# Moving the query norm's factor from the rotated queries into the softmax exponent

## The chip, the cores and the metric

One NeuronCore of a Trainium2 chip runs the whole program. The metric is the device time of one execution in microseconds, as the median of several runs; one further execution is recorded by the hardware profiler. Lower is better.

## The reference

A two-layer hybrid network over 512 latent tokens and 256 context tokens of width 1024. The first layer mixes with grouped-query attention (16 query heads, 4 key heads, head width 64), the second with a gated linear recurrence; each is followed by a SwiGLU network. The part that matters here:

```python
def rms_norm(x, w):
    xf = x.astype(jnp.float32)
    y = xf * lax.rsqrt(jnp.mean(xf * xf, axis=-1, keepdims=True) + NORM_EPS)
    return (y * w.astype(jnp.float32)).astype(x.dtype)
...
    def queries(h):
        q = (h @ w_q).reshape(b, t, ATTN_KV_HEADS, ATTN_GROUP, HEAD_DIM).transpose(0, 2, 3, 1, 4)
        return rms_norm(q, q_norm)
    q_l = apply_axial_rope(queries(h_lat), rope)
...
def gqa_attend(q, k, v):
    s = jnp.einsum('bkgqd,bksd->bkgqs', q, k) * (HEAD_DIM ** -0.5)
    p = jax.nn.softmax(s, axis=-1).astype(v.dtype)
    return jnp.einsum('bkgqs,bksd->bkgqd', p, v)
```

The factor `rsqrt(mean(q*q)+eps)` is one number for each token and head. Weight, rotation and the product with the keys are linear in the query, so the number can be applied to the scores of that token and head instead.

## The kernel before, in words

All products with weights are done in three passes (`mm3`, lines 112 to 114): high part times high part, high times low, low times high. A weight tile is loaded raw, cast to its high part on ScalarE (line 88) and its low part is the difference, mostly on VectorE (line 91). For the query weights there are three buffers of each part, and two tiles for each of four groups of heads.

**Query projection.** For each of 4 groups of heads and each of 3 pairs of token tiles (`tp`), 48 matmuls fill one PSUM bank with 128 tokens x 2 x 4 heads x 64. Four such banks rotate. `q_first` then normalises, rotates and splits the queries; its `second` transposes them on TensorE (line 592) and casts them into `qT` (line 595, ScalarE) three calls later. In group 0 the same work for the keys (`k_first`) stands between. `qk_norm_rope` squares the bank on ScalarE (line 510), sums per head on VectorE (513), and makes the factor from a scale-and-add (514), a square root on ScalarE (515), a reciprocal and one refinement step (516 to 520), all on 128x8. It writes the normalised queries `qhat` (522), one buffer only. The rotation is two VectorE products with the cosines (532), four GpSimd products with the sines (537) and a sum (541); context tokens (`tp == 2`) have one product with the weight (526). A cast (585) and a difference (586) give the two parts of the transposed operand.

**Attention.** 96 units, one for each head and tile of 128 tokens. A unit is: scores on TensorE into one of two PSUM buffers `s2` (645, 646), the negated row maximum on VectorE (689), the exponential with that maximum as bias and its sum on ScalarE (691), the reciprocal of the sum on VectorE (692), the scaling of the 128x768 probabilities on GpSimd (693). Three units later the probabilities are transposed on TensorE (703) and split into two parts on ScalarE (88) and VectorE (91); six units later they meet the values (714, 715). The products with the output weights of the group before and other small work fill in between. GpSimd also makes the low parts of the output weights and of the attention outputs (91).

The order on each engine is set when the program is built, by program order and readiness; each engine then runs its list in order.

Of the kernel before, what the change touches and what calls it, by code (L numbers as in the profile page):

```python
# [8 lines left out]
F32 = mybir.dt.float32  # L9
F32R = mybir.dt.float32r  # L10
U8 = mybir.dt.uint8
AF = mybir.ActivationFunctionType
ALU = mybir.AluOpType
AX = mybir.AxisListType
PSUM = bass.MemoryType.PSUM

P = 128
# [5 lines left out]
NT = T // P  # L23
NLT = NL // P
EPS = 1e-6
HEADS = 16
KVH = 4
HD = 64
# [19 lines left out]
def kernel(  # L48
# [10 lines left out]
    PE, DVE, ACT, POOL = nc.tensor, nc.vector, nc.scalar, nc.gpsimd  # L59
# [20 lines left out]
    def bank(name):  # L80
        return psums["pool"].tile([P, 512], F32, tag="b", bufs=psums["bufs"]["b"], name=name)
# [97 lines left out]
    def ada_mm(pa, mv, k):  # L179
        for j, m in enumerate(mv):  # L180
            PE.matmul(pa[32 * j : 32 * (j + 1)], cpad[:, k], m, start=(k == 0), stop=(k == KT - 1))

    def ada_put(pa, rows, dst, bias, nch, nk):
        n = nch * nk * 32
        w = min(n, P)
        ACT.copy(rows[0:w, 0 : max(n, P)], pa[0:w])
        pt = bank("pta")
        for i in range(0, n, P):
            PE.transpose(pt[:, i : i + w], rows[0:w, i : i + P], ident[0:w, 0:w])
        cols = pt[:, 0:n].rearrange("p (c k r) -> p c k r", c=nch, r=32)[:, :, :, 0:2]  # L190
        DVE.tensor_tensor(dst, cols, bias.unsqueeze(3).to_broadcast([P, nch, nk, 2]), op=ALU.add)
# [5 lines left out]
    def ada_chunk(ch, pa, rows, load):  # L197
        pa = (bank("pa") if pa is None else pa)[:, 0:256]
        for k in range(KT):
            raw = load(f"adw{ch}{k}")  # L200
            dma(raw, ada_w[0, k * P : (k + 1) * P, ch * D : (ch + 1) * D])
            r4 = raw.rearrange("p (b j n) -> p b j n", b=2, j=4)
            ada_mm(pa, [r4[:, :, j] for j in range(4)], k)
            yield
        ada_put(pa, rows(), modc[0][:, ch : ch + 1], ada_bias(0, ch, 1), 1, KT)
# [123 lines left out]
    qst = pool("qkvst", qes, side="right")  # L329
# [41 lines left out]
    for t in range(NT):  # L371
        r = rs0[:, t : t + 1]
# [44 lines left out]
    for k in range(KT):  # L417
        ps = s2(f"ptx{k}")
        for t in range(NT):
            PE.transpose(ps[:, t * P : (t + 1) * P], xt[t][:, k * P : (k + 1) * P], ident)  # L420
        h = stp.tile([P, T], F32, name=f"xhT{k}")
        if k % 2:
            ACT.copy(h, ps[:, 0:T])
        else:
# [3 lines left out]
    kraw = [qst.tile([P, 2, 256], F32, tag="kraw" if tp else "qsin", bufs=2 if tp else 1, name="kraw")  # L428
            for tp in range(NT // 2)]
# [38 lines left out]
    keep = pool("attkeep", att)  # L468
# [3 lines left out]

    qT = [qt_tile(g) for g in range(KVH)]
    kTt = keep.tile([P, 2 * KVH, T], F32R, name="kT")
    kTh = [kTt[:, g] for g in range(KVH)]
    kTl = [kTt[:, KVH + g] for g in range(KVH)]

# [4 lines left out]
    tabs = {}  # L482
    for nm, wsrc, sc in (("k", attn_k_norm, 1.0), ("q", attn_q_norm, HD ** -0.5)):
        w = qst.tile([P, HD], F32, name=f"w{nm}")
# [3 lines left out]
        cw = qst.tile([P, NLT, HD], F32, name=f"cw{nm}")  # L488
        sw = qst.tile([P, NLT, HD], F32, name=f"sw{nm}")
# [10 lines left out]
        tabs[nm] = (w, cw, sw)  # L500

    def qk_norm_rope(src, tp, nm, eng=POOL):
        w, cw, sw = tabs[nm]

        def tmp(tag, bufs=1):
            tt = qst.tile([P, 512], F32, tag=tag, bufs=bufs, name=tag)
            return tt.rearrange("p (t h d) -> p t h d", t=2, d=HD)

        sq = tmp("qrot", 2)
        ACT.activation(sq, src, AF.Square)  # L510
        sst = qst.tile([P, 3, 8], F32, tag="ss", bufs=2, name="ss")
        ss, sr, sa = sst[:, 0], sst[:, 1], sst[:, 2]
        DVE.tensor_reduce(ss, sq.rearrange("p t h d -> p (t h) d"), op=ALU.add, axis=AX.X)
        DVE.tensor_scalar(ss, ss, 1.0 / HD, EPS, op0=ALU.mult, op1=ALU.add)
        ACT.activation(sr, ss, AF.Sqrt)
        DVE.reciprocal(sr, sr)
        DVE.tensor_tensor(sa, sr, sr, op=ALU.mult)
        DVE.tensor_tensor(sa, sa, ss, op=ALU.mult)
        DVE.tensor_scalar(sa, sa, -0.5, 1.5, op0=ALU.mult, op1=ALU.add)
        DVE.tensor_tensor(ss, sr, sa, op=ALU.mult)  # L520
        qh = tmp("qhat")
        DVE.tensor_tensor(qh, src, ss.rearrange("p (t h) -> p t h", t=2).unsqueeze(3).to_broadcast([P, 2, 4, HD]),
                          op=ALU.mult)
        r = tmp("qrot", 2)
        if tp == 2:
            eng.tensor_tensor(r.rearrange("p t h d -> p (t h) d"), qh.rearrange("p t h d -> p (t h) d"),
                               w.unsqueeze(1).to_broadcast([P, 8, HD]), op=ALU.mult)
            return r
        sn = tmp("qsin")
        for tt in range(2):  # L530
            t = tp * 2 + tt
            DVE.tensor_tensor(r[:, tt], qh[:, tt], cw[:, t].unsqueeze(1).to_broadcast([P, 4, HD]), op=ALU.mult)
            sn5 = sn[:, tt].rearrange("p h (a b i) -> p h a b i", a=2, b=2)
            q5 = qh[:, tt].rearrange("p h (a b i) -> p h a b i", a=2, b=2)
            t5 = sw[:, t].rearrange("p (a b i) -> p a b i", a=2, b=2)
            for b in range(2):
                POOL.tensor_tensor(
                    sn5[:, :, :, b], q5[:, :, :, 1 - b],
                    t5[:, :, b].unsqueeze(1).to_broadcast([P, 4, 2, 16]), op=ALU.mult,
                )  # L540
        DVE.tensor_tensor(r, r, sn, op=ALU.add)
        return r
# [8 lines left out]
    def k_first(tp):  # L551
# [26 lines left out]

        return second

    def q_first(g, tp, ps):
        eng = DVE if g == KVH - 1 and tp == 2 else POOL
        r = qk_norm_rope(ps.rearrange("p (t h d) -> p t h d", t=2, d=HD), tp, "q", eng)
        qd = qst.tile([P, 2, 4, 2, HD], F32R, tag="sp", bufs=3, name="qd")
        DVE.tensor_copy(qd[:, :, :, g % 2], r)
        eng.tensor_tensor(qd[:, :, :, 1 - g % 2], r, qd[:, :, :, g % 2].bitcast(F32), op=ALU.subtract)

        def second():
            for tt in range(2):
                pt = bank("ptq")  # L590
                for j in range(4):
                    PE.transpose(pt[:, j * P : (j + 1) * P],
                                 qd[:, tt, j].rearrange("p a d -> p (a d)").bitcast(F32), ident)
                t = tp * 2 + tt
                ACT.copy(qT[g][:, :, t * P : (t + 1) * P], pt.rearrange("p (h t) -> p h t", h=4))

        return second
# [3 lines left out]
    apsum = psums["pool"].tile([P, 512], F32, tag="a", name="pa")  # L601
# [2 lines left out]
        return psums["pool"].tile([P, 512], F32, tag="q", bufs=psums["bufs"]["q"], name=name)  # L604

    dfill = Fill()
    dfill.add(ada_chunk(3, apsum, lambda: qst.tile([P, 256], F32, tag="arows", name="arows"), ring_raw))
    later = []

    def first(fn, *args):  # L610
        if len(later) == Q_LAG:
            later.pop(0)()
        later.append(fn(*args))

    pend = []
    for g in range(KVH):
        ws = []
        for i in range(2):
            src = attn_w_qkv[0, 512 * i : 512 * (i + 1), g * 256 : (g + 1) * 256].rearrange("(k p) n -> p k n", p=P)
            ws.append(load_split(src, [P, 4, 256], f"wq{g}{i}"))  # L620
        for tp in range(3):
            psf = qbank(f"q{g}{tp}")
            for tt in range(2):
                ts_ = slice((tp * 2 + tt) * P, (tp * 2 + tt + 1) * P)
                ks = list(range(KT)) if tt == 0 else list(range(4, KT)) + list(range(4))
                for k in ks:
                    wh, wl = ws[k // 4]
                    mm3(psf[:, tt * 256 : tt * 256 + 256], hn_hi[k][:, ts_], hn_lo[k][:, ts_],
                        wh[:, k % 4], wl[:, k % 4], k == ks[0], k == ks[-1])
            if g == 0:  # L630
                first(k_first, tp)
            first(q_first, g, tp, psf[:, 0:512])
            dfill.step(2)
    def key_tiles(t):
        return range(4, 6) if t >= NLT else range(NT)

# [46 lines left out]
    def scores(h, t):  # L683
        ps = early.pop((h, t), None)
        if ps is None:
            ps = score_mm(h, t)
        nk = len(key_tiles(t)) * P
        st3 = ap_.tile([P, 4], F32, tag="st3", bufs=4, name="st3")
        DVE.tensor_reduce(st3[:, 0:1], ps[:, :nk], op=ALU.max, axis=AX.X, negate=True)  # L689
        pf = ap_.tile([P, T], F32, tag="pf", bufs=4, name="pf")[:, :nk]  # L690
        ACT.activation(pf, ps[:, :nk], AF.Exp, bias=st3[:, 0:1], accum_out=st3[:, 1:2])  # L691
        DVE.reciprocal(st3[:, 2:3], st3[:, 1:2])  # L692
        POOL.tensor_scalar(pf, pf, st3[:, 2:3], 1.0, op0=ALU.mult, op1=ALU.mult)  # L693
        return pf
# [947 lines left out]
    sa, sb = scan_head(GH - 2), scan_head(GH - 1)  # L1642
# [73 lines left out]
```

## Time and profile before

| | before |
|---|---|
| median of 3 runs | 1841.82 us (1838.89 to 1844.04) |
| profiled execution: time, span | 1841.11 us, 1839.3 us |
| mean granted TensorE clock | 0.989 of 2.4 GHz |
| TensorE / VectorE / ScalarE / GpSimd busy | 96% / 72% / 46% / 37% of the span |
| query projection | from 76 to about 175 us |
| attention | from about 179 to 422 us |

Busy time is the sum of an engine's own instructions; a busy TensorE is not one at its peak, since its matmuls overlap. The 1.8 us between the profiled time and the span lie outside the program's instructions.

### The profile page before, as it was taken

To read this page: it belongs to the slowest core of one execution; us is meant where nothing else is said; L and a number is where in the kernel's file an instruction comes from. 1 tells how busy PE (TensorE), PEld (TensorE's weight loads), DVE (VectorE), ACT (ScalarE), POOL (GpSimd) and SP (SyncE) were. 2 spreads that over 40 slices of the span, in tenths; PEclk is the share of its full clock that TensorE was granted. 3 is DMA by queue.
4 is the path that set the end of the run, shared out by engine and by line. 5 is a ranking of instruction groups with operands and counts; after the bars stand their busy time and mean duration, and the time that the engine had idled before them with its cause. 6 is when DMAs were issued, how large, how long until landed. Compare 5 with 4: busy or idle time off the path is not lost.

```text
span 1839.3 us, 30682 instructions
## 1 busy us (share of the span) xinstructions
PE 1758.3 (96%) x11725; PEld 1606.6 (87%) x11725; DVE 1327.1 (72%) x2315; ACT 844.0 (46%) x1752; POOL 680.5 (37%) x609
## 2 busy tenths in 40 slices
PE   8989999999999999999999999999998889999997
PEld 6779678988899989898998979899897789999996
DVE  3576688888888788877766465665747698786764
ACT  4333787777533424242445323233333455554544
POOL 1244255445513314131315353344537254443420
PEclk9989999999999999999999999999999999999999
DMA  9433510002034243535331111122211123333322
GB/s 328 163 114 86 161 65 24 12 13 75 24 110 125 64 126 92 160 116 155 103 104 57 58 58 55 61 81 83 78 47 46 44 61 111 108 105 105 98 60 82
DMA packets 213458, 166.43 MB, mean 90 GB/s; under 512 B 7952, under 2 KB 190400, under 8 KB 213312
## 3 DMA queue, kind: packets, MB, share of 16 engines
q1 hardware_dynamic: 213024, 163.43, 29.1%
q8 instruction: 92, 1.51, 0.3%
q10 hardware_dynamic: 288, 1.05, 0.1%
q14 instruction: 54, 0.44, 0.1%
HBM read 162.36 MB, written 2.10 MB: 89 GB/s over the span
## 4 chain that ended last, share of the span: by engine, by line
PE 77%; DVE 11%; POOL 4%; ACT 4%; issue 2%; DMA 1%; POOLq 0%; SPq 0%; ACTq 0%; DVEq 0%
PE ffo L113 5%; PE ffo L114 5%; PE ffo L112 5%; PE x L112 4%; PE x L113 4%; PE x L114 4%; PE pt L703 3%; PE y L114 2%; PE y L112 2%; PE y L113 2%; PE lv L1504 2%; PE hz L112 2%; PE hz L113 2%; PE hz L114 2%; PE sc L645 1%
## 5 line engine op out<-in xcount | busy, mean ns | idle before, releaser
L1511 POOL TENSOR_TENSOR KD<-KD,tot 128x384 f32<-128x384 f32 x96 | 100.5, 1070 | 67.0 <-ACT kc L1494 65.4
L693 POOL TENSOR_SCALAR pf<-pf,st 128x768 f32<-128x768 f32 (+1 forms) x96 | 73.4, 767 | 128.1 <-DVE st L692 91.7
L676 DVE SCALAR_TENSOR_TENSOR hT<-ffo,modc,hT 128x512 f32<-128x512 f32 (+1 forms) x122 | 78.7, 650 | 53.3 <-PE ffo L114 53.3
L114 PE MATMUL ffo<-gh,wlo_w 128*128 128x512 f32 (+1 forms) x304 | 103.8, 342 | 0.0
L113 PE MATMUL ffo<-gl,whi_w 128*128 128x512 f32 (+1 forms) x304 | 103.5, 341 | 0.0
L112 PE MATMUL ffo<-gh,whi_w 128*128 128x512 f32 (+1 forms) x304 | 102.5, 340 | 0.0
L1494 ACT COPY kc<-KD 128x256 f32<-128x256 f32 x112 | 42.9, 413 | 102.4 <-POOL KD L1511 37.1
L91 DVE TENSOR_TENSOR ptl<-pt,pth 128x384 fp32r<-128x384 f32 (+1 forms) x160 | 79.8, 524 | 12.5 <-ACT pth L88 11.2
L235 DVE SCALAR_TENSOR_TENSOR adacc<-adw,csil,adacc 128x512 f32<-128x512 f32 x98 | 84.6, 873 | 5.0 <-DMA adw<-in_ada_w_dram 4.7
L1511 DVE TENSOR_TENSOR QD<-QD,tot 128x256 f32<-128x256 f32 x96 | 57.1, 635 | 41.2 <-PE lv L1504 40.5
L88 ACT CAST pth<-pt 128x384 fp32r<-128x384 f32 (+1 forms) x160 | 69.9, 461 | 34.3 <-PE pt L703 22.5
L689 DVE TENSOR_REDUCE st<-sc 128x1 f32<-128x768 f32 (+1 forms) x96 | 74.2, 773 | 15.3 <-PE sc L646 12.5
L691 ACT ACTIVATE pf<-sc,st 128x768 f32<-128x768 f32 (+1 forms) x96 | 73.4, 765 | 19.2 <-DVE st L689 18.3
L703 PE MATMUL pt<-ident,pf 128*128 128x128 f32 x448 | 72.2, 275 | 5.1 <-DVE ptl L91 3.8
L112 PE MATMUL ffo<-gh,foh 128*128 128x512 f32 (+1 forms) x186 | 71.5, 384 | 0.0
L113 PE MATMUL ffo<-gl,foh 128*128 128x512 f32 (+1 forms) x186 | 71.0, 382 | 0.4 <-DVE gl L91 0.4
L114 PE MATMUL ffo<-gh,fol 128*128 128x512 f32 (+1 forms) x186 | 70.8, 381 | 0.0
L1504 PE MATMUL lv<-QD,kc 128*128 128x128 f32 x448 | 64.2, 288 | 5.7 <-DVE QD L1511 2.5
L1504 PEld LDWEIGHTS lv<-QD,kc 128*128 128x128 f32 x448 | 59.1, 194 | 10.1 <-issue 4.7
L113 PEld LDWEIGHTS ffo<-gl,whi_w 128*128 128x128 f32 x304 | 58.3, 192 | 7.1
L114 PEld LDWEIGHTS ffo<-gh,wlo_w 128*128 128x128 f32 x304 | 58.2, 191 | 6.6
L703 PEld LDWEIGHTS pt<-ident,pf 128*128 128x128 f32 x448 | 51.3, 140 | 14.4 <-issue 6.6
(1104 smaller groups left out, 6777.2 us busy)
## 6 DMA issues: line engine op xcount, KB each, us to landing
adw<-in_ada_w_dram SPq DMA_DIRECT2D x40, 512.0 KB, 4.5
adw<-in_ada_w_dram SPq DMA_DIRECT2D x80, 256.0 KB, 2.8
raw_hz<-in_hgrn_w_in_dram SPq DMA_DIRECT2D x14, 512.0 KB, 3.8
adr<-in_ada_w_dram SPq DMA_DIRECT2D x16, 256.0 KB, 4.5
adr<-in_ada_w_dram SPq DMA_DIRECT2D x8, 512.0 KB, 6.6
raw_wq<-in_attn_w_qkv_dram SPq DMA_DIRECT2D x8, 512.0 KB, 4.8
raw_wo<-in_attn_w_o_dram SPq DMA_DIRECT2D x8, 512.0 KB, 3.6
raw_hv<-in_hgrn_w_in_dram SPq DMA_DIRECT2D x8, 512.0 KB, 4.5
```

What stands on the lines that cost most here:

```text
L91: (eng or DVE).tensor_tensor(lo, src, hi.bitcast(F32), op=ALU.subtract)
L112: PE.matmul(ps, ahi, bhi, start=first, stop=False, **kw)
L113: PE.matmul(ps, ahi, blo, start=False, stop=False, **kw)
L114: PE.matmul(ps, alo, bhi, start=False, stop=last, **kw)
L235: pin(DVE.scalar_tensor_tensor(a, raw, cc, a, op0=ALU.mult, op1=ALU.add))
L676: DVE.scalar_tensor_tensor(hT[o][:, a:e], ps, mcol(layer, ch, o, v), hT[o][:, a:e], op0=ALU.mult, op1=ALU.add)
L689: DVE.tensor_reduce(st3[:, 0:1], ps[:, :nk], op=ALU.max, axis=AX.X, negate=True)
L691: ACT.activation(pf, ps[:, :nk], AF.Exp, bias=st3[:, 0:1], accum_out=st3[:, 1:2])
L693: POOL.tensor_scalar(pf, pf, st3[:, 2:3], 1.0, op0=ALU.mult, op1=ALU.mult)
L703: PE.transpose(pt[:, i * P : (i + 1) * P], pf[:, (i0 + i) * P : (i0 + i + 1) * P], ident)
L1504: PE.matmul(ps[:, cs], kc[:, cs], mv, start=True, stop=True)
L1511: eng.tensor_tensor(view, view, f, op=ALU.mult)
```

## The change

For the queries, the normalised copy is gone. ScalarE copies the raw bank to SBUF (`raw`, in the one buffer of `qhat`) and squares it; VectorE sums the squares of each head into a kept table `rq`. The rotation works on the raw values: VectorE multiplies straight from PSUM with the cosines, GpSimd multiplies the copy with the sines. The seven small steps that make the factor from the sum are done once per group of heads on 128x6x4 (`q_scales`), after the first tile of the next group. In attention each unit has one more VectorE product, of the 128x1 negated maximum with the 128x1 factor, and the exponential takes that as its bias and the factor as its scale, a second per-partition operand. The keys go as before. Two small tiles share other buffers.

```diff
+    rq = keep.tile([P, NT, HEADS], F32, name="rq")
...
+        return rope(qh, tp, nm, eng)
+
+    def rope(qh, tp, nm, eng, raw=None):
+        w, cw, sw = tabs[nm]
+        raw = qh if raw is None else raw
...
-            eng.tensor_tensor(r.rearrange("p t h d -> p (t h) d"), qh.rearrange("p t h d -> p (t h) d"),
+            eng.tensor_tensor(r.rearrange("p t h d -> p (t h) d"), raw.rearrange("p t h d -> p (t h) d"),
...
-            q5 = qh[:, tt].rearrange("p h (a b i) -> p h a b i", a=2, b=2)
+            q5 = raw[:, tt].rearrange("p h (a b i) -> p h a b i", a=2, b=2)
...
+    def q_scales(g):
+        ss = rq[:, :, 4 * g : 4 * g + 4]
+        sr = qst.tile([P, 2, NT, 4], F32, tag="sr", name="sr")
+        sr, sa = sr[:, 0], sr[:, 1]
+        DVE.tensor_scalar(ss, ss, 1.0 / HD, EPS, op0=ALU.mult, op1=ALU.add)
+        ACT.activation(sr, ss, AF.Sqrt)
+        DVE.reciprocal(sr, sr)
+        DVE.tensor_tensor(sa, sr, sr, op=ALU.mult)
+        DVE.tensor_tensor(sa, sa, ss, op=ALU.mult)
+        DVE.tensor_scalar(sa, sa, -0.5, 1.5, op0=ALU.mult, op1=ALU.add)
+        DVE.tensor_tensor(ss, sr, sa, op=ALU.mult)
...
-        r = qk_norm_rope(ps.rearrange("p (t h d) -> p t h d", t=2, d=HD), tp, "q", eng)
+        src = ps.rearrange("p (t h d) -> p t h d", t=2, d=HD)
+        raw = qst.tile([P, 512], F32, tag="qhat", name="qraw")
+        ACT.copy(raw, ps)
+        sq = qst.tile([P, 512], F32, tag="qrot", bufs=2, name="sqq")
+        ACT.activation(sq, ps, AF.Square)
+        mine = rq[:, 2 * tp : 2 * tp + 2, 4 * g : 4 * g + 4]
+        DVE.tensor_reduce(mine, sq.rearrange("p (t h d) -> p t h d", t=2, d=HD), op=ALU.add, axis=AX.X)
+        if tp == 2:
+            pend.append(g)
+        r = rope(src, tp, "q", eng, raw.rearrange("p (t h d) -> p t h d", t=2, d=HD))
...
-    dfill.add(ada_chunk(3, apsum, lambda: qst.tile([P, 256], F32, tag="arows", name="arows"), ring_raw))
+    dfill.add(ada_chunk(3, apsum, lambda: qst.tile([P, 512], F32, tag="kraw", bufs=2, name="arows"), ring_raw))
...
+            if pend and tp == 0:
+                q_scales(pend.pop(0))
             dfill.step(2)
+    q_scales(pend.pop(0))
...
-        ACT.activation(pf, ps[:, :nk], AF.Exp, bias=st3[:, 0:1], accum_out=st3[:, 1:2])
+        scale = rq[:, t, h : h + 1]
+        DVE.tensor_tensor(st3[:, 3:4], st3[:, 0:1], scale, op=ALU.mult)
+        ACT.activation(pf, ps[:, :nk], AF.Exp, bias=st3[:, 3:4], scale=scale, accum_out=st3[:, 1:2])
```

## Rows read from the trace of the kernel before

**Rows 1.** Windows: stretch, busy (instructions) by engine, clock, DMA share, GB/s.

```profile
128.00:135.00 7.00, 1.86 (x16) 1.66 (x14) 5.51 (x12) 3.81 (x6) 3.29 (x5) 0.79 0.00 0
135.00:141.00 6.00, 6.00 (x37) 6.00 (x38) 4.01 (x10) 0.21 (x1) 2.45 (x3) 0.68 0.58 178
175.00:187.00 12.00, 8.46 (x67) 6.64 (x65) 6.99 (x14) 6.64 (x11) 1.28 (x1) 0.86 1.02 262
```

**Rows 2.** Waits, 76 to 182 us: total us, times, longest.

```profile
ACT ss L515 <- DVE ss L514: 32.8, 13, 4.8
...
PE q L113 <- DVE wlo_wq L91: 5.1, 1, 5.1
...
PE sc L645 <- DVE qhat L522: 3.5, 1, 3.5
...
PE pta L189 <- ACT kT L571: 1.8, 1, 1.8
...
PE ptk L567 <- ACT qT L595: 1.5, 1, 1.5
```

**Rows 3.** Timeline around the longest wait: start, duration, engine, line, operation.

```profile
128.26 1.05 ACT L88 CAST whi_wq<-raw_wq 128x1024 fp32r<-128x1024 f32 x1
...
133.61 1.22 DVE L91 TENSOR_TENSOR wlo_wq<-raw_wq,whi_wq 128x1024 fp32r<-128x1024 f32 x1
```

**Rows 4.** Timeline at the passage from projection to attention.

```profile
179.01 0.50 PE L645 MATMUL sc<-kT,qT 128*128 128x512 f32 x1 [3.54 <-DVE qhat L522]
...
186.24 0.90 ACT L691 ACTIVATE pf<-sc,st 128x768 f32<-128x768 f32 x1
```

**Rows 5.** VectorE groups by form, 76 to 182 us: busy, mean ns | idle before.

```profile
L522 DVE TENSOR_TENSOR qhat<-q,ss 128x512 f32<-128x512 f32 x12 | 8.3, 692 | 1.0
...
L517 DVE TENSOR_TENSOR ss<-ss 128x8 f32<-128x8 f32 x15 | 3.8, 252 | 0.5
```

**Rows 6.** Windows of the attention stage, four of 60 us.

```profile
181.00:241.00 60.00, 57.84 (x438) 42.65 (x437) 37.05 (x84) 45.61 (x99) 21.41 (x24) 0.98 0.55 169
241.00:301.00 60.00, 57.27 (x395) 51.32 (x394) 51.98 (x118) 44.42 (x107) 26.83 (x29) 1.00 0.06 19
301.00:361.00 60.00, 59.08 (x418) 53.92 (x417) 52.99 (x122) 45.13 (x107) 26.78 (x28) 1.00 0.06 19
361.00:421.00 60.00, 59.08 (x417) 53.85 (x416) 52.55 (x121) 45.64 (x110) 28.10 (x29) 1.00 0.07 19
```

**Rows 7.** VectorE in attention, 181 to 422 us: a group, then a wait.

```profile
L692 DVE RECIPROCAL st<-st 128x1 f32<-128x1 f32 x96 | 15.0, 157 | 15.6 <-ACT pf L691 14.9
...
DVE st L692 <- ACT pf L691: 14.9, 20, 1.6
```

**Rows 8.** Timeline of VectorE and GpSimd around 91 us.

```profile
91.15 1.25 DVE L517 TENSOR_TENSOR ss<-ss 128x8 f32<-128x8 f32 x1
92.44 0.17 DVE L518 TENSOR_TENSOR ss<-ss 128x8 f32<-128x8 f32 x1
92.64 0.17 DVE L519 TENSOR_SCALAR ss<-ss 128x8 f32<-128x8 f32 x1
...
91.09 1.30 POOL L586 TENSOR_TENSOR qd<-qrot,qd 128x512 fp32r<-128x512 f32 x1 [1.27 <-DVE qd L585]
```

**Rows 9.** GpSimd groups in attention, 181 to 422 us.

```profile
L693 POOL TENSOR_SCALAR pf<-pf,st 128x768 f32<-128x768 f32 (+1 forms) x94 | 72.5, 773 | 128.1 <-DVE st L692 91.7 <-PE pt L703 32.9 <-PE rx L671 1.4
L91 POOL TENSOR_TENSOR wlo_wo<-raw_wo,whi_wo 128x1024 fp32r<-128x1024 f32 x8 | 19.1, 2389 | 9.1 <-ACT whi_wo L88 9.1
L91 POOL TENSOR_TENSOR qT<-ofp,qT 128x768 fp32r<-128x768 f32 x4 | 7.4, 1842 | 2.0 <-ACT qT L88 2.0
L91 POOL TENSOR_TENSOR o<-ofp,o 128x768 fp32r<-128x768 f32 x3 | 5.5, 1847 | 1.9 <-ACT o L88 1.9
```

**Rows 10.** ScalarE by form, 1500 to 1840 us: with and without a per-partition scale.

```profile
L835 ACT ACTIVATE fy<-hT,cols 128x512 f32<-128x512 f32 x6 | 4.3, 713 | 0.0
...
L267 ACT ACTIVATE sq<-hT 128x512 f32<-128x512 f32 x5 | 3.2, 637 | 0.0
```

More of the change, by code (lines that the diff above doesn't have):

```diff
@@ L502, in qk_norm_rope @@
     def qk_norm_rope(src, tp, nm, eng=POOL):
-        w, cw, sw = tabs[nm]
         def tmp(tag, bufs=1):
@@ L523, in qk_norm_rope, with tmp @@
                           op=ALU.mult)
+        return rope(qh, tp, nm, eng)
+    def rope(qh, tp, nm, eng, raw=None):
+        w, cw, sw = tabs[nm]
+        raw = qh if raw is None else raw
+        def tmp(tag, bufs=1):
+            tt = qst.tile([P, 512], F32, tag=tag, bufs=bufs, name=tag)
+            return tt.rearrange("p (t h d) -> p t h d", t=2, d=HD)
         r = tmp("qrot", 2)
         if tp == 2:
-            eng.tensor_tensor(r.rearrange("p t h d -> p (t h) d"), qh.rearrange("p t h d -> p (t h) d"),
+            eng.tensor_tensor(r.rearrange("p t h d -> p (t h) d"), raw.rearrange("p t h d -> p (t h) d"),
                                w.unsqueeze(1).to_broadcast([P, 8, HD]), op=ALU.mult)
```

## The prediction

> **What bounds the kernel now.** The table of engines says TensorE, busy for 96% of the span, but that average hides two different stages that the change touches, so I read them separately.
>
> For the projection (76 to 175 us) I read the waits first. TensorE waits little, and in four places only: 5.1 us for the low part of a weight tile, 3.5 us before the first scores, 1.8 and 1.5 us for transposition banks that ScalarE had not yet emptied [rows 2]. The timeline gives the cause of the first: ScalarE had the high part of the tile finished at 129.3, but VectorE made the low part only at 133.61 [rows 3], because it was working off older query tiles. The other side is that ScalarE lost 32.8 us in its square roots, waiting in order for VectorE's small steps [rows 2]. So VectorE runs behind in this stage, and TensorE pays for it in a few places. The windows add a second price: in the 6 us after the long wait TensorE ran at a granted clock of 0.68, between its 1.2 and its 2.4 GHz [rows 1].
>
> For attention (about 181 to 422 us) I read the windows. In the last three windows of 60 us TensorE is busy for 57.3 to 59.1 us, VectorE for 52.0 to 53.0, ScalarE for about 45 and GpSimd for 27 to 28 [rows 6]. TensorE sets the pace, and VectorE has only 8.0, 7.0 and 7.4 us of idle time in each window. 96 units in 240 us are 2.5 us a unit, or 24 to a window. The reader is to see that this stage has two nearly full engines.
>
> **The projection, part by part.** For each of 12 query tiles VectorE loses the 128x512 product `qhat`, 0.69 us [rows 5], and six small steps of 128x8 that take 0.17 to 0.25 us each when nothing else happens [rows 5, 8], some 1.8 us in all, or 22 us in the stage. `q_scales` gives back 4 x 6 small steps of about 0.2 us, 5 us, which lie beside matmuls. The two cosine products now read PSUM; their size is the same, and I take their cost as unchanged. ScalarE gains a 128x512 copy for each tile; its nearest row is a 128x512 pass of 0.64 us [rows 10], 12 x 0.64 = 7.7 us, and loses 8 of 12 square roots with their waits (32.8 us for queries and keys together [rows 2]). The copy has to wait until GpSimd is done with the one buffer `qhat`, but GpSimd starts earlier now, since the sines wait for a copy and no longer for the factor. I cost these moves at nothing: the cover is ScalarE's waiting time, and without it 7.7 us would be the price of the copies.
>
> What TensorE gets back:
> - The 5.1 us wait. The high part still comes only at 129.3 (its buffer is freed by the group before), and the low part takes 1.22 us more [rows 3]. TensorE came to a halt 5.1 us before the low part's end at 134.83, at 129.7. If VectorE is free, it resumes at about 130.6: 0.9 us are left, 4.2 are gained. Without the halt the low clock goes too: 6 us at 0.68 are 1.9 us of work not done [rows 1]. Together 6.1.
> - The waits of 1.8 and 1.5 us, where ScalarE's evictions stand behind a square root: I take 2.5 of 3.3.
> - The passage to attention. The scores stood still for 3.54 us until `qhat` had read the last bank, at 179.0 [rows 4]. Now ScalarE's copy and square are the last readers for a context tile, about 1.3 us after the last matmul, so this wait goes. The queries' last operand is also ready some 4 to 5 us earlier, and the first exponential, at 186.24 [rows 4], follows it. TensorE idles for 3.5 of the 12 us from 175 to 187, at a clock of 0.86 [rows 1]. I take 4.5.
>
> Sum: 6.1 + 2.5 + 4.5 = 13.1 us. Bounds: 7 if the rest of the list lets VectorE still come late half of the time, 17 if all waits and the low clock go (5.1 + 3.5 + 1.8 + 1.5 + 1.9, and 3 for the clock and the earlier start at the passage).
>
> **Attention, part by part.** The exponential gets a second per-partition operand. The nearest rows are a 128x512 pass with a per-partition scale, 0.713 us, and one without, 0.637 [rows 10]: 0.08 us, 96 times, 7 us of ScalarE, which has 15 us idle in each window [rows 6]. I cost it at nothing; without that cover it is 7 us.
>
> VectorE gets 96 products of 128x1. The lower bound is the row of its reciprocal on the same shape, 0.157 us [rows 7]; steps that follow each other start 0.20 us apart [rows 8]. So 24 x 0.20 = 4.8 us in a window that has 7.0 to 8.0 idle [rows 6]. That alone fits.
>
> The upper bound comes from one row. A 128x8 product with both inputs in SBUF, L517, usually takes 0.17 us; at 91.15 it took 1.25 and ended at 92.40, just when GpSimd's L586, begun at 91.09, ended at 92.39 [rows 8]. The mean over its 15 is 0.252 [rows 5]. The new product is of this kind: maximum and factor both lie in SBUF. VectorE's large steps in attention (maximum, split, residual) have an input in PSUM, and the reciprocal has one input and kept its 0.157 us in the mean over 96 [rows 7], so VectorE has not paid for GpSimd in this stage so far.
>
> The Trainium skill, page "SBUF — State Buffer", section "Who interferes with whom", says the same as a rule: a VectorE instruction with two SBUF inputs shares a read path with GpSimd instructions that read SBUF, and the second to start waits for the whole of the first. The row of L517 agrees (1.25 us). By that rule the product waits whenever GpSimd is at work; by the row of the reciprocal it would not, and the sum would be the 13 us gain alone.
>
> Price of the waiting: a product that starts at a random moment meets, on the average, the sum over GpSimd's instructions of busy time times half their length, over 240 us [rows 9]: 72.5 x 0.39 + 19.1 x 1.19 + 7.4 x 0.92 + 5.5 x 0.92 = 62.9, so 0.26 us. With 0.20 for the step itself 0.46 us a unit, 11.0 us in a window.
>
> What stands behind the product on VectorE: the exponential of its own unit, and all that VectorE has next, the splits that TensorE's products with the values need and the reciprocals that GpSimd waits for (91.7 us of its waits end so [rows 9]). A score buffer is held until the exponential has read it, and there are two.
>
> How much is hidden: in the first window VectorE has 23 us idle, and I cost the products there at nothing. In the other three they need 11.0 each, against 8.0, 7.0 and 7.4 of idle time [rows 6]: 3.0 + 4.0 + 3.6 = 10.6 us over, if every idle moment can be used. If none can, it is 33. Much of the idle time can't: 14.9 us of it are reciprocals that wait for an exponential [rows 7], which starts later now. I take the middle, 22.
>
> **Sum.** Against the profiled execution of 1841.1 us, 0.7 below the median of the runs: 1841.1 - 13.1 + 22 = 1850. With the ends of both terms: 1841.1 - 17 + 10.6 = 1835 to 1841.1 - 7 + 33 = 1867.
>
> **Rivals.**
> - *Faster: the product finds its place.* The product isn't held by GpSimd at this size, or falls into moments when GpSimd rests. For it: GpSimd is busy for only 45% of a window [rows 6], and with 0.20 us a unit everything fits. Against it: L517's row. It decides below some 0.29 us a unit (24 x 0.29 = 7.0, the least idle window). Then only the gain is left: 1841.1 - 13.1 = 1828. Chance 0.20.
> - *No difference: the idle time takes most of it.* The products wait as costed, but VectorE's idle moments absorb them: +10.6 against -13.1, 1839. For it: TensorE has lists of other work (output weights) to go on with. Against it: VectorE's waits for ScalarE, which grow with it. Chance 0.27.
> - *Much slower: VectorE becomes the bound.* No idle time is usable and TensorE, halted for GpSimd's 2.39 us pieces, falls to its lower clock at times: 1841.1 - 13.1 + 33 = 1861 and above. Chance 0.10.
>
> My forecast, slower by about 8 us, has 0.43.
>
> **The numbers.** 0.3% of 1841.8, 5.5 us, is about what a measurement of this kernel can tell from no change; that is 1836.3 to 1847.3. Faster takes the first rival and a little of the second, 0.22; slower takes the forecast and the last rival without their low edges, 0.51; the same gets 0.27. The predicted time is 1850. The likeliest case alone spans 1844 to 1858. For 8 in 10 I go down to the faster rival, 1828, and up to 1862, leaving out about 0.1 at either end.
>
> **What would show it.** Right: in the profile after, the wait for the low part at 129.7 is below 1.5 us, ScalarE's square roots number 4 for the queries, the scores begin within 1 us of the last projection, and attention starts about 10 us earlier. Then in attention the new 128x1 product has a mean of 0.35 us or more, with single ones over 1 us that end when a GpSimd instruction ends; VectorE is busy for over 57 of 60 us, and TensorE's idle time grows. Wrong: the product's mean stays near 0.17 us and attention keeps its 240 us, or the order of the lists moves so that the waits of the projection come back elsewhere.

## The result: 0.3% slower, two changes that nearly cancel

The changed kernel takes 1846.91 us in the median of its runs (1842.87 to 1852.34) against 1841.67 for the kernel before in the same rounds: a ratio of 1.0029, with a 95% interval of 1.0019 to 1.0038. The forecast was 1850.

Behind the small number stand two large ones. From the first exponential to the last, the kernel before went from 186.2 to 421.8 us, 235.6 us; the changed one goes from 172.7 to 427.9, 255.2 us. Attention begins 13.5 us earlier and lasts 19.6 us longer. In the table "way" is the mean, over the 96 units, of the time from the end of a maximum to the start of its exponential, worked out from the single instructions of each trace; it is one of the two main witnesses below; the other is what TensorE waits for.

| | before | after |
|---|---|---|
| first exponential, us | 186.2 | 172.7 |
| attention, us | 235.6 | 255.2 |
| way, us | 0.39 | 1.02 |

**Projection after.** The windows that answer to [rows 1]:

```profile
128.00:135.00 7.00, 7.00 (x62) 7.00 (x61) 4.90 (x11) 2.79 (x6) 3.13 (x6) 1.00 0.46 149
135.00:141.00 6.00, 6.00 (x54) 6.00 (x53) 1.91 (x5) 2.07 (x4) 3.04 (x5) 1.00 0.00 1
```

TensorE is busy without a break where it had stood still for 5.1 us, and its granted clock is 1.00 where it was 0.79 and 0.68. The waits from 76 to 175 us, TensorE's first and then some of ScalarE's, answer to [rows 2]:

```profile
PE ptk L576 <- ACT qT L625: 2.5, 1, 2.5
PE q L112 <- DVE cols L463: 0.6, 1, 0.6
PE sc L678 <- ACT sqq L608: 0.5, 1, 0.5
...
ACT sr L595 <- DVE rq L594: 7.9, 4, 3.1
...
ACT qraw L606 <- POOL qd L616: 4.5, 1, 4.5
...
ACT qraw L606 <- POOL qrot L535: 2.7, 1, 2.7
```

No wait for a low part is left, ScalarE waits for 4 square roots of the queries (`sr`), and in their place stand single waits of the raw copy for GpSimd. One of TensorE's small waits has grown, from 1.5 to 2.5 us. The passage in the timeline (start, duration, engine, line, operation, idle time before), for [rows 4]:

```profile
166.86 0.50 PE L678 MATMUL sc<-kT,qT 128*128 128x512 f32 x1 [0.48 <-ACT sqq L608]
...
172.72 0.99 ACT L726 ACTIVATE pf<-sc,st,rq 128x768 f32<-128x768 f32 x1
```

The first scores wait 0.48 us instead of 3.54 and come 12.2 us earlier.

**Attention after.** Four windows of 60 us that end, as those of [rows 6] do, within 1 us of the stage's end:

```profile
187.00:247.00 60.00, 52.64 (x390) 40.76 (x389) 48.30 (x121) 46.16 (x106) 26.80 (x27) 1.00 0.36 115
247.00:307.00 60.00, 57.16 (x380) 50.02 (x381) 52.56 (x129) 41.57 (x95) 24.09 (x25) 1.00 0.06 19
307.00:367.00 60.00, 57.55 (x383) 50.38 (x384) 52.63 (x135) 43.70 (x99) 25.95 (x27) 1.00 0.04 10
367.00:427.00 60.00, 57.31 (x382) 50.01 (x379) 51.89 (x134) 43.46 (x99) 23.55 (x25) 1.00 0.03 10
```

TensorE is busy for 0.1, 1.5 and 1.8 us less in the last three windows than in those of [rows 6], and for 5.2 less in the first, which begins 14 us after the first exponential where that of [rows 6] begins 5 us before it. VectorE, third of the busy columns, is at 52 to 53 us in the last three, where it was before: it has more to do for each unit, units pass more slowly, and the two cancel. By the prediction's account it would be at 57 and more. The same over the whole stage, before and after:

```profile
186.20:421.80 235.60, 228.59 (x1632) 197.99 (x1625) 194.26 (x441) 177.39 (x419) 103.93 (x109) 1.00 0.17 52
172.70:427.90 255.20, 237.83 (x1636) 200.09 (x1629) 214.47 (x537) 186.66 (x419) 105.40 (x110) 1.00 0.16 52
```

TensorE's idle time has grown from 7.0 to 17.4 us; the rest of the 19.6 us shows as busy time of the same matmuls. VectorE works 20.2 us longer in a stage that is 19.6 us longer. These sums alone would fit an engine whose idle moments can't be used at all; one of the experiments below separates that from the other reading. What TensorE waits for is told by two rows, one of its weight loads (PEld) and one of its matmuls, before and then after: the scores wait until an exponential (`pf`) has read the score buffer, and the transpositions wait until VectorE's split (`ptl`) has read their bank.

```profile
PEld sc L645 <- ACT pf L691: 3.1, 9, 0.9
PE pt L703 <- DVE ptl L91: 3.4, 7, 1.1
...
PEld sc L678 <- ACT pf L726: 9.1, 22, 1.5
PE pt L738 <- DVE ptl L91: 7.5, 16, 1.1
```

Below they are called the score wait and the split wait. Loads and matmuls overlap, so the two don't add up to the loss; they show where it arises. The new product, as one line's instructions (shortest, median, longest ns), with those that waited for it, and then ScalarE's exponentials by form (busy, mean ns of one, idle time before them):

```profile
L725 DVE TENSOR_TENSOR st<-st,rq x96: 136/158/1594, 170.6 to 426.7; 128x1 f32<-128x1 f32 x96
...
  ACT pf L726: 34.4, 49
  POOL pf L728: 18.7, 12
```

```profile
L726 ACT ACTIVATE pf<-sc,st,rq 128x768 f32<-128x768 f32 x64 | 63.7, 995 | 33.0 <-DVE st L725 32.0 <-DVE st L727 0.9
```

The same group before, over its attention:

```profile
L691 ACT ACTIVATE pf<-sc,st 128x768 f32<-128x768 f32 x64 | 58.0, 906 | 17.6 <-DVE st L689 16.8 <-DVE st L692 0.3
```

The exponential is 0.089 us longer (995 - 906 ns), and ScalarE's wait ahead of the large ones has gone from 17.6 to 33.0 us. Two stretches of the timeline show what it waits for. First, GpSimd holds the product:

```profile
219.61 2.40 POOL L91 TENSOR_TENSOR wlo_wo<-raw_wo,whi_wo 128x1024 fp32r<-128x1024 f32 x1 [0.67 <-ACT whi_wo L88]
...
221.26 0.76 DVE L725 TENSOR_TENSOR st<-st,rq 128x1 f32<-128x1 f32 x1
...
222.12 0.99 ACT L726 ACTIVATE pf<-sc,st,rq 128x768 f32<-128x768 f32 x1 [0.54 <-DVE st L725]
```

The product ends at 222.02, GpSimd's piece at 222.01. Second, the product stands in VectorE's list behind a split that has nothing to do with it, and is then held as well:

```profile
284.06 0.95 DVE L722 TENSOR_REDUCE st<-sc 128x1 f32<-128x768 f32 x1
...
284.12 1.84 POOL L91 TENSOR_TENSOR qT<-ofp,qT 128x768 fp32r<-128x768 f32 x1
...
284.93 0.55 DVE L91 TENSOR_TENSOR ptl<-pt,pth 128x384 fp32r<-128x384 f32 x1
...
285.39 0.58 DVE L725 TENSOR_TENSOR st<-st,rq 128x1 f32<-128x1 f32 x1
...
286.07 0.99 ACT L726 ACTIVATE pf<-sc,st,rq 128x768 f32<-128x768 f32 x1 [1.24 <-DVE st L725]
```

The maximum is done at 285.01 and its exponential starts at 286.07. The split accounts for 0.38 us of that (the product starts at 285.39), and GpSimd's piece, which ends at 285.96, for most of the product's 0.58. In 87 of the 96 units some other step of VectorE stands between maximum and product (37 times one split, 19 times a reciprocal and a split), and the product starts 0.41 us after the maximum's end in the mean.

### The profile page after: what moved, and what is told of

Same layout as the page of the kernel before. It is cut to its first block, busy times and chain, and to the rows that moved or that the text cites. A ratio compares the mean times of both kernels' runs of the same rounds, so it can differ in the third digit from the quotient of the medians.

```text
span 1846.6 us, 30777 instructions
## 1 busy us (share of the span) xinstructions
PE 1765.2 (96%) x11725; PEld 1606.8 (87%) x11725; DVE 1326.5 (72%) x2351; ACT 856.9 (46%) x1756; POOL 678.9 (37%) x609
## 4 chain that ended last, share of the span: by engine, by line
PE 75%; DVE 13%; ACT 4%; POOL 3%; issue 3%; DMA 1%; SPq 0%; POOLq 0%; ACTq 0%; DVEq 0%
PE ffo L113 5%; PE ffo L114 5%; PE ffo L112 5%; PE x L112 4%; PE x L114 4%; PE x L113 4%; PE y L114 2%; PE y L112 2%; PE y L113 2%; PE lv L1539 2%; PE hz L112 2%; PE hz L113 2%; PE hz L114 2%; PE pt L738 2%; DVE QD L1546 1%
## 5 line engine op out<-in xcount | busy, mean ns | idle before, releaser
L726 ACT ACTIVATE pf<-sc,st,rq 128x768 f32<-128x768 f32 (+1 forms) x96 | 81.9, 853 | 35.8 <-DVE st L725 34.4
```

What stands on the lines that cost most here:

```text
L726: ACT.activation(pf, ps[:, :nk], AF.Exp, bias=st3[:, 3:4], scale=scale, accum_out=st3[:, 1:2])
```

## The experiments

Two theories. *VectorE's capacity*, that of the prediction: the products, lengthened by waiting for GpSimd, use up VectorE's idle time, and what doesn't fit is the loss. *The longer way*: VectorE has the time, but the score buffer, of which there are two, is held longer for each unit, because a second step, its place in the list and its waits lie between maximum and exponential. Each run was timed in 5 rounds beside the kernel before on the same chip, whose median there was 1841.4 to 1842.9 us, so the ratios are what is compared. A ratio is taken over all runs and can differ a little from the quotient of the medians (0.9918 for "no factor"). All of them:

| kernel | median us | ratio to before (95%) | attention us | way us |
|---|---|---|---|---|
| before | 1841.7 | 1 | 235.6 | 0.39 |
| after | 1846.9 | 1.0029 (1.0019 to 1.0038) | 255.2 | 1.02 |
| no factor | 1826.3 | 0.9910 (0.9897 to 0.9923) | 234.2 | 0.36 |
| operand only | 1828.1 | 0.9921 (0.9908 to 0.9934) | 236.5 | 0.35 |
| step off the chain | 1833.6 | 0.9954 (0.9940 to 0.9969) | 240.1 | 0.39 |
| one-input step | 1840.8 | 0.9993 (0.9984 to 1.0002) | 248.6 | 0.96 |
| product on ScalarE | 1845.5 | 1.0013 (1.0003 to 1.0022) | 251.8 | 0.86 |
| before with product | 1860.8 | 1.0107 (1.0089 to 1.0124) | 255.1 | 1.07 |
| product tied, one input | 1846.4 | 1.0029 (1.0018 to 1.0039) | 254.4 | 1.01 |
| product tied | 1855.7 | 1.0078 (1.0063 to 1.0093) | 263.4 | 1.17 |
| fixed list, no step | 1839.5 | 0.9985 (0.9973 to 0.9997) | 246.2 | 0.35 |
| fixed list, one input | 1845.5 | 1.0020 (1.0009 to 1.0030) | 252.3 | 0.53 |
| fixed list, product | 1854.4 | 1.0063 (1.0049 to 1.0076) | 263.0 | 0.64 |
| scale fused with maximum | 1830.4 | 0.9937 (0.9924 to 0.9949) | 239.2 | 0.35 |

**The two halves apart.** The changed kernel without the factor, then with the operand alone:

```diff
-        DVE.tensor_tensor(st3[:, 3:4], st3[:, 0:1], scale, op=ALU.mult)
-        ACT.activation(pf, ps[:, :nk], AF.Exp, bias=st3[:, 3:4], scale=scale, accum_out=st3[:, 1:2])
+        ACT.activation(pf, ps[:, :nk], AF.Exp, bias=st3[:, 0:1], accum_out=st3[:, 1:2])
     # second kernel: ..., bias=st3[:, 0:1], scale=ones[:, 0:1], accum_out=...
```

> The changed kernel without the 128x1 product and without the second operand of the exponential; the queries' norm factor is left out of the scores, the projection and the four factor computations stay. All theories that put the loss into the product or the operand expect the gain of the projection alone: 1841.7 - 13.5 = about 1828 us, with attention again about 236 us from the first to the last exponential. If the loss comes from the changed projection itself (its lists pushed into attention), it stays above 1840.

> The changed kernel without the 128x1 product, but with a second per-partition operand (a column of ones) in the exponential; the norm factor is left out of the scores. GpSimd theory (the product waits for GpSimd): within 3 us of the run without both, about 1829. Rival, ScalarE's operand (0.09 us on each of 96 exponentials, on the path): most of the loss remains, 1840 or more.

Measured 1826.3 and 1828.1. The projection's part is thus worth 0.9% of the time (0.0090 x 1841.7 = 16.6 us), and the operand's price, 0.0011 x 1841.7 = 2.0 us, is not clear of the two intervals. ScalarE's cover holds: 96 longer exponentials cost next to nothing.

The other way round, the product put into the kernel before:

```diff
-        ACT.activation(pf, ps[:, :nk], AF.Exp, bias=st3[:, 0:1], accum_out=st3[:, 1:2])
+        DVE.tensor_tensor(st3[:, 3:4], st3[:, 0:1], ones[:, 0:1], op=ALU.mult)
+        ACT.activation(pf, ps[:, :nk], AF.Exp, bias=st3[:, 3:4], scale=ones[:, 0:1], accum_out=st3[:, 1:2])
```

> The kernel before, whose queries are normalised, with a product of 128x1 by a column of ones on VectorE and that column as the exponential's second operand, so that only attention's part of the change is made. If the two parts add up: 1841.4 + 19 to 21 = about 1861. If the product only costs when attention starts early: 1850 or less.

Measured 1860.8, attention 255.1 us: 19.5 us more than before, as in the changed kernel. The halves add up within the intervals, and neither needs the other to explain it.

**GpSimd's share.** The product is replaced by a step of the same size that reads one input of SBUF:

```diff
-        DVE.tensor_tensor(st3[:, 3:4], st3[:, 0:1], scale, op=ALU.mult)
+        DVE.tensor_reduce(st3[:, 3:4], st3[:, 0:1], op=ALU.max, axis=AX.X)
     # and scale=ones[:, 0:1] in the exponential
```

> In place of the 128x1 product with two inputs in SBUF a VectorE maximum of 128x1 with one input, same place in the list, and a column of ones as the exponential's second operand; the norm factor is left out of the scores. GpSimd theory: the step takes 0.16 us every time, the 12 us of waiting for GpSimd go, and with them 8 us or more of the time: 1832 to 1838. Rival, the step itself (a further link between maximum and exponential, whatever its inputs): no change, 1845 to 1848.

The step's line in this kernel:

```profile
L725 DVE TENSOR_REDUCE st<-st x96: 125/144/155, 168.3 to 417.9; 128x1 f32<-128x1 f32 x96
```

None of the 96 is late, against 24 products over 0.3 us and the longest of 1594 ns after. Yet the time falls only from a ratio of 1.0029 to 0.9993, 6.6 us; 13.3 us (0.9993 against 0.9921) are left for a step that takes 0.14 us and waits for nobody. That is nearly all of its 96 x 0.14 = 14 us, as if not one of VectorE's idle moments, over 7 us in each window, could take it. Either that is so, or the price is that of the way.

**Time or way.** The same kernel with one word changed, so that nobody waits for the step:

```diff
-        ACT.activation(pf, ps[:, :nk], AF.Exp, bias=st3[:, 3:4], scale=ones[:, 0:1], ...)
+        ACT.activation(pf, ps[:, :nk], AF.Exp, bias=st3[:, 0:1], scale=ones[:, 0:1], ...)
```

> As the kernel with the one-input step and the operand of ones (1840.8 us), so without the factor, but the exponential takes the maximum itself as its bias: the step is still issued 96 times on VectorE and nobody waits for its result. If what the step costs is VectorE's time, 96 x 0.14 = 14 us less than VectorE's idle moments take up, the time stays near 1841. If it is the longer way from a maximum to its exponential, the time falls to that of the kernel with the operand alone, 1828 to 1831, and the mean way is 0.35 to 0.4 us again instead of 0.96.

Measured 1833.6, between the two. VectorE's list still has another step between maximum and step in 87 of 96 units, as with the one-input step, though not always the same one: a split alone in 51 units instead of 37. The windows over the whole attention of three kernels, operand only, step off the chain, one-input step:

```profile
172.70:409.00 236.30, 228.90 (x1631) 198.19 (x1623) 195.62 (x441) 184.07 (x417) 104.28 (x109) 1.00 0.18 56
```

```profile
173.00:413.30 240.30, 230.28 (x1636) 198.67 (x1636) 202.73 (x536) 185.62 (x418) 104.66 (x110) 1.00 0.17 56
```

```profile
170.50:418.90 248.40, 235.13 (x1634) 199.49 (x1623) 202.26 (x537) 186.41 (x417) 105.03 (x110) 1.00 0.17 54
```

The second and the third do the same work: VectorE is busy for 202.7 and 202.3 us in 536 and 537 instructions. The third takes 8.1 us longer, and what was changed is that its exponential waits for the step (it also begins 2.9 us earlier, so it ends only 5.6 us later). This is the run that tells the theories apart: of the step's 13.3 us, 7.2 (0.9993 - 0.9954) come with the longer way, and 6.1 (0.9954 - 0.9921) are there without it, through VectorE's time or the shifted lists, which this run doesn't separate.

Two more readings bear this out. From the first line to the second VectorE's busy time grows by only 7.1 us, since neighbouring records overlap; so even with no idle moment of use its time could hardly account for 13.3. And TensorE's score wait is 3.2 us with the operand alone, 3.8 with the step off the chain and 8.7 with the step on it, so it is indeed the score buffer that comes free later. The split wait stays at 3.5 to 4.3 in all three and grows to 7.5 only in the changed kernel, whose products GpSimd holds: that part makes VectorE late for its splits. A third score buffer would test the longer way directly; no run has one.

**Off VectorE altogether.** The product as a ScalarE copy with a scale:

```diff
-        DVE.tensor_tensor(st3[:, 3:4], st3[:, 0:1], scale, op=ALU.mult)
+        ACT.activation(st3[:, 3:4], st3[:, 0:1], AF.Copy, scale=scale)
```

> The product is made by ScalarE (a copy with the factor as scale), everything else as in the changed kernel. GpSimd theory: VectorE is as loaded as before the change, ScalarE has 96 x 0.2 = 19 us more in a stage where it idles for a quarter; 1828 to 1835, faster than both kernels. Rival, the longer link between maximum and exponential: the step on ScalarE is as long as on VectorE and the loss stays, 1843 or more.

Measured 1845.5, not measurably better than the changed kernel (1.0003 to 1.0022 against 1.0019 to 1.0038). VectorE has its time back and GpSimd can't hold this step, but the copy takes 0.296 us in the median and the way is 0.86 us. It fits the longer way: the score wait is 9.6 us, as in the changed kernel, and the split wait 2.7, below that of the kernel before. But ScalarE also has 28 us (96 x 0.296) more to do.

**The product's place in the list.** If the split ahead of the product is half of the way, a product right behind its maximum should win that back. First attempt: the other steps of VectorE in attention are made to follow the product in the order, and the reciprocal moves to the next unit:

```diff
-        DVE.tensor_tensor(st3[:, 3:4], st3[:, 0:1], scale, op=ALU.mult)
+        prod.append(DVE.tensor_tensor(st3[:, 3:4], st3[:, 0:1], scale, op=ALU.mult))
...
-        DVE.reciprocal(st3[:, 2:3], st3[:, 1:2])
+        norm_prev()          # the reciprocal and GpSimd's product of the unit before
...
+            behind(DVE.tensor_tensor(ptl[:, i0 : i0 + n, qs], src, hi.bitcast(F32), op=ALU.subtract))
```

> The changed kernel, with VectorE's other attention steps tied behind the product, so that the product stands right behind its maximum in VectorE's list; the reciprocal and scaling of a unit are written one unit later. List theory (in the changed kernel 75 of 96 products stand behind another VectorE step, mostly a split, 0.41 us in the mean, and the exponential waits for that): 0.4 us less between maximum and exponential and 6 to 12 us off the time, 1835 to 1841. Rival, the step alone: unchanged, 1845 or more.

> The same lists with the one-input VectorE maximum of 128x1 in place of the product, and a column of ones as the exponential's second operand; the norm factor is left out of the scores. List theory together with GpSimd theory: both delays are gone, only 0.16 us of step are left; 1829 to 1834. Rival, the step alone: 1840.

Measured 1855.7 and 1846.4. The attempt failed in its aim: in 50 of 96 units another step still stood in between, and the way was 1.17 us. It says nothing on the place. The pair does say again what GpSimd costs: 9.0 us (1.0078 - 1.0029).

Second attempt: the order of VectorE's steps in attention is fixed outright, as they are written, with the step right behind its maximum:

```diff
-        DVE.tensor_reduce(st3[:, 0:1], ps[:, :nk], op=ALU.max, axis=AX.X, negate=True)
-        DVE.tensor_tensor(st3[:, 3:4], st3[:, 0:1], scale, op=ALU.mult)
+        pin(DVE.tensor_reduce(st3[:, 0:1], ps[:, :nk], op=ALU.max, axis=AX.X, negate=True))
+        pin(DVE.tensor_tensor(st3[:, 3:4], st3[:, 0:1], scale, op=ALU.mult))
     # splits, sums, residuals and the reciprocal (behind the next maximum) are pinned too;
     # the one-input step in place of the product, or no step, in the other two
```

> VectorE's attention steps are fixed in one order (maximum of a unit, reciprocal of the unit before, splits, the rest), without the 128x1 step, with a column of ones as the exponential's second operand; the norm factor is left out of the scores. This is the base for the next two. If the order is as good as the free one, 1828; if it is worse by itself, up to 1845.

> The same fixed order with the one-input VectorE maximum of 128x1 right behind each unit's maximum, nothing between; the norm factor is left out of the scores. List theory (the place in the list made the step dear): 0 to 5 us more than the run without the step, since only 0.2 us are added between maximum and exponential. Rival, any separate step costs its 12 us: 10 us or more.

> The same fixed order with the real product right behind each maximum. GpSimd theory: 4 to 9 us more than with the one-input step, with single products over 1 us that end with a GpSimd instruction; list theory: in sum faster than the changed kernel's 1846.9 if the fixed order is not worse by itself. Rival to GpSimd: the same as the one-input step.

The first of them shows that the fixed order is itself 11.8 us worse (0.9985 against 0.9921) than the list it replaces, so it is no remedy. Inside it the place is right: the step starts 0.03 us behind the maximum, and the way grows by 0.18 us only. The step then costs 6.4 us (1.0020 - 0.9985), where it cost 13.3 in the free list. That a bad place is about half of the step's price is argued from this, not shown, since the two lists differ in everything else. The real product costs another 7.9 us (1.0063 - 1.0020). In these lists the loss arises at another place: the split wait is 6.9 us without the step, 13.4 with it and 21.3 with the product, while the score wait is 4.8, 4.2 and 6.6. So with a way of only 0.53 to 0.64 us the step and the product still cost 14 us in sum, and what grows is TensorE's wait for VectorE's splits, as the theory of VectorE's capacity has it. The product's line:

```profile
L731 DVE TENSOR_TENSOR st<-st,rq x96: 159/160/1778, 170.3 to 432.9; 128x1 f32<-128x1 f32 x96
```

**No step at all.** The factor can be applied while the maximum is taken, by one instruction that multiplies the scores in place in PSUM and keeps the least of the products; the factor gets a minus sign in `q_scales`, so the least is the negative of the greatest:

```diff
-        DVE.tensor_reduce(st3[:, 0:1], ps[:, :nk], op=ALU.max, axis=AX.X, negate=True)
-        DVE.tensor_tensor(st3[:, 3:4], st3[:, 0:1], scale, op=ALU.mult)
-        ACT.activation(pf, ps[:, :nk], AF.Exp, bias=st3[:, 3:4], scale=scale, accum_out=st3[:, 1:2])
+        DVE.tensor_scalar(ps[:, :nk], ps[:, :nk], rq[:, t, h : h + 1], None, op0=ALU.mult, op1=ALU.min,
+                          accum_out=st3[:, 0:1])
+        ACT.activation(pf, ps[:, :nk], AF.Exp, bias=st3[:, 0:1], scale=-1.0, accum_out=st3[:, 1:2])
```

> No separate step: the maximum over the scores is replaced by one VectorE instruction that multiplies the scores in PSUM with minus the factor, writes them back and keeps their minimum; the exponential takes that minimum as bias and minus one as scale. If the loss comes from the separate step in any of its forms (place in the list, waiting for GpSimd, length) the gain of the projection stays whole: 1825 to 1832, below both kernels. If writing 768 scores back to PSUM makes the instruction longer than the maximum's 0.95 us by more than 0.15 us, 1835 or more.

Its line, by instruction:

```profile
L723 DVE TENSOR_SCALAR_CACHE_REDUCE sc<-sc,rq x96: 475/1015/1027, 169.1 to 409.7; 128x768 f32<-128x768 f32 x64, 128x256 f32<-128x256 f32 x32
L723 DVE DVE_READ_ACCUMULATOR sc<-sc,rq x96: 82/141/145, 170.1 to 410.1; 128x1 f32 x96
```

Measured 1830.4, a ratio of 0.9937 (0.9924 to 0.9949): it beats both kernels, with the factor applied. The read of the accumulator follows at once, so nothing gets in between; the way is 0.35 us, and the longest instruction is 12 ns above the median, so GpSimd doesn't hold it. The exponential has no second per-partition operand here, so the kernel without the factor is the one to compare: some 5 us of the gain are paid for the longer pass (0.9937 against 0.9910), in which VectorE's instruction with its read takes 0.2 us more than the maximum.

## Why the prediction came out right, and which step did not

Sums below are differences of ratios times 1841.7 us; by the intervals of the two ratios each has 2 to 4 us of uncertainty either way.

**The projection, 13.1 us predicted.** The first exponential is 13.5 us earlier, and without the factor the kernel is 16.6 us faster. Term by term: the wait for the low part was to shrink to 0.9 us and is gone, and the clock is 1.00, as predicted. The passage: the wait of 3.54 us is 0.48. Of the two waits for transposition banks, one has gone (1.8) and one has grown to 2.5, so of the 2.5 us predicted there at most 0.8 are seen (1.8 + 1.5 - 2.5). The moves costed at nothing, copies and square roots, can't have cost much, as the start shows, though the copies do wait for GpSimd's use of their one buffer (4.5 and 2.7 us).

The cosine products were taken as unchanged. They are shorter. Shortest, median and longest ns of the 16 of the queries, before and after, and then of the 4 of the keys after:

```profile
L532 DVE TENSOR_TENSOR qrot<-qhat,cwq x16: 419/682/725, 87.6 to 172.4; 128x256 f32<-128x256 f32 x16
...
L541 DVE TENSOR_TENSOR qrot<-q,cwq x16: 405/415/426, 85.7 to 161.2; 128x256 f32<-128x256 f32 x16
...
L541 DVE TENSOR_TENSOR qrot<-qhat,cwk x4: 415/555/691, 79.1 to 91.4; 128x256 f32<-128x256 f32 x4
```

The shape is the same. With both inputs in SBUF, 10 of the 16 took 680 to 725 ns, each of them while GpSimd multiplied the same `qhat` with the sines, and the other six 419 to 426; the keys' after fall into the same two kinds, two and two. With one input in PSUM all 16 take 405 to 426, also the three that ran beside a product with the sines. So GpSimd no longer delays them, which is worth 2.8 us of VectorE's time.

**Attention, 22 us predicted, 19.6 measured, by the wrong road.** The step of the prediction that failed is "how much is hidden": products of 0.46 us a unit against VectorE's idle time, of which the step's own 0.20 us were to fit and the waiting for GpSimd was to overflow. The own 0.20 us did not fit: a step of 0.14 us that nothing holds costs 13.3 us. The waiting for GpSimd is real but half as long: the mean product took 0.28 us, 0.12 above the median of 0.158, where 0.26 of waiting was predicted. Its group in the profile after:

```profile
L725 DVE TENSOR_TENSOR st<-st,rq 128x1 f32<-128x1 f32 x96 | 26.9, 280 | 0.6
```

The estimate took a random moment, and that was right: GpSimd was at work when 41 of the 96 products started (43%; it is busy for 41% of the stage), and the rest of its instruction was 0.246 us in the mean over all 96, against 0.26 estimated. Two other things were not. A held product ends with GpSimd's instruction (all 24 products over 0.3 us do), so its own 0.158 us lie inside the waiting and do not come on top, as the row of L517 in the prediction already had it: 0.05 us in the mean. And eight products that started 0.07 to 0.08 us after a scaling of GpSimd's were not held at all, 0.07 in the mean. One of them:

```profile
195.66 0.92 POOL L728 TENSOR_SCALAR pf<-pf,st 128x768 f32<-128x768 f32 x1 [2.39 <-DVE st L727]
...
195.73 0.15 DVE L725 TENSOR_TENSOR st<-st,rq 128x1 f32<-128x1 f32 x1
```

The witness that the prediction named, a mean of 0.35 us or more, is missed, and so is the other, VectorE busy for over 57 of 60 us. Singles over 1 us that end with a GpSimd instruction are there, and TensorE's idle time has grown.

What the runs put in its place, for 21.9 us from no factor (0.9910) to the changed kernel (1.0029): 2.0 for the operand, 6.1 for a step that nobody waits for, 7.2 for the exponential's waiting for it, 6.6 for GpSimd's holding it. 13.3 of the 21.9 us are there with a step of 0.14 us that no engine disturbs. The prediction did list the exponential as standing behind the product, but gave that no price, and it took the product to follow its maximum at once, while in 87 of 96 units another step came first. That the 6.1 us are VectorE's time is likely, since the fused kernel pays 5 us for as much added busy time (194.3 to 201.5 us) and no added wait, but not shown.

The Trainium skill, page "SBUF — State Buffer", section "Who interferes with whom", has VectorE with two SBUF inputs share a read path with GpSimd, and VectorE with one input go free. These runs agree: the product at up to 1594 ns, the one-input step of the same size at 155 at most. The rule that the prediction took from there, that the second to start waits for the whole of the first, holds for the 24 late products and not for the eight above; there the measurement decides.

**The rivals.** "Faster, the product finds its place" needed less than 0.29 us a unit; the product took 0.28 and the kernel was slower all the same, so its condition was the wrong one. "The idle time takes most of it" was 8 us too low. "VectorE becomes the bound" missed its 1861, and TensorE's granted clock stayed at 1.00. Its condition, that no idle moment is of use, is not refuted by VectorE's 52 us in 60, but by the step off the chain: the same busy time in a stage that is 8.1 us shorter. That the total came within about 3 us of the forecast is in part luck: the 22 was the middle between two ends, and met the 21.9 with a waiting that was twice too long and a step that was to cost nothing. The 3 us that it missed by are about what the projection gave beyond its forecast (16.6 against 13.1).

## What to carry to other kernels

A step of 0.15 us that is added between the filling of a buffer and its release costs by what it adds to the way, its place in the list and its waits included, and not only by its busy time: here 96 of them cost 20 us on an engine that showed the same busy share as before, and about a third of that was there when nobody waited for them. Look whether a busy share can hide the work, and separately whether a result is awaited; a kernel in which the step is done and nobody waits for it tells the two apart. If the factor must be applied, look for an instruction that already passes over the data and can take it along.

## What was not expected of the hardware

- The accumulating form of VectorE's multiplication reads and writes PSUM in place at 1.015 us for 128x768, and its accumulator's read takes 0.141 us; the maximum alone takes about 0.95 us. The longest multiplication of the 96 was 1.027 us, so none of them was held by GpSimd.
- A product of 128x1 that usually takes 0.158 us took up to 1.594 us (1.778 in the fixed list), ten times as long, when GpSimd had begun first. But eight of the ten products that started within 0.1 us of the start of a GpSimd instruction took 0.136 to 0.150 us.
- A product of 128x256 with both inputs in SBUF took either about 0.42 us or 0.68 to 0.73 beside GpSimd's products; with one input in PSUM it never took more than 0.426.
